# A two-layer decoder trunk on one core: two gate products of the second layer move into the gap between two attentions

## The chip, the cores and the metric

The kernel runs on one core of one Trainium2 chip. The time is device microseconds from start to end of one launch. Three runs of the kernel before took 914.35, 915.20 and 915.77 us; the median is 915.2 us. One further execution was recorded by the hardware profiler; all rows below come from it.

## The reference

Two layers run over 256 tokens of width 1024, in f32. Each layer has a mixer with three branches that are gated and summed, and a feed-forward part:

```
h = modulate(rms_norm(x, mix_norm_g), sh1, sc1)
z = h @ w_in      # MLA latents | MoBA q, k, v | conv input | 3 gates of 1024
o_a = causal_attention(q_full, k_full, v_a) @ w_mla_o          # 8 heads
o_b = moba_attention(q_b, k_b, v_b) @ w_moba_o                 # 8 heads of 64, rope
o_c = silu(layer_norm(causal_dwconv31(u))) @ w_conv_pw2 + b
g = sigmoid(gates)
x = x + g1 * ((g[0]*o_a + g[1]*o_b + g[2]*o_c) @ w_out)
h = modulate(rms_norm(x, ffn_norm_g), sh2, sc2)
x = x + g2 * channel_mixer(h, w_up, w_dw, w_down)
```

With 256 tokens and blocks of 256, MoBA has one block, so its attention is causal attention over 256 keys. The gates depend on `h` alone, so their products can run at any time after `h` is there. The convolution over 31 tokens also depends on `h` alone.

## The kernel before

Weights arrive as 128x1024 f32 tiles of 512 KB (a *unit*). SP issues the load; ACT copies the tile into `whi` in a shorter format (line 219) and DVE subtracts that from the original to get `wlo` (line 221). A product of two f32 matrices is then three products: `whi` with the high part of `h` (`hh`, line 297), `whi` with its low part (`hl`, line 298), and `wlo` with `hh` (line 300). One unit gives 8 + 8 + 8 = 24 matrix products of 128x256 on PE, accumulated in a PSUM bank. `raw`, `whi` and `wlo` have 4 buffers each; up to three units are split ahead of the one in use. PSUM banks: five of tag `psa`, three of `psb`.

The order of the mixer's work is written out by hand in the table `STEPS` (one string for each layer, line 77 on), as a list of short names. The instructions of a name are issued when it is reached, and the ones of neighbouring names are then interleaved on each engine when the program is built; the result is one fixed list for each engine, and each engine works through its list in order. The names that matter here:

- `C20`, `C21`: the two halves (units) of pair 2 of the third gate, 24 products each (`gate_c`); after the second half ACT takes the tanh (line 788). `C10`, `C11`, `C30`, `C31` are the pairs beside it.
- `G00`, `G01`, `G10`, ...: the same for the first two gates (`gate_ab`).
- `MA13`, `MA14`, ...: steps of the MLA attention of the second half of the heads; `BA00`..`BA03` and `BA10`..`BA13`: steps of the MoBA attention of the two halves of its heads. Both go through `attn4`: scores and mask on PE (lines 605, 607, 610, 613), maxima on DVE (619, 622, 628), exponentials on ACT (641), reciprocal on DVE (646), scaling on ACT (653), transposes on PE (662) with copies on ACT (665), products with the values on PE (674), and the output's high and low parts on ACT (677) and DVE (678).
- `BP0`, `BP1`: rope of the MoBA queries and keys of the two blocks of 128 tokens (`moba_prep`): DVE lines 965, 588, 589 and 972, then eight transposes on PE (line 976) into two banks and two copies on ACT (line 977) into `qkTb`. No MoBA score can be computed before both blocks are there.
- `O0`, `O1`, ...: output products of MLA and MoBA (`out_ab`), with `obl`, the low part of the MoBA output (line 678), in their last products; DVE lines 1126 and 1129 follow.
- `LN`: the mean of the convolution's output (`conv_mean`): three DVE sums (lines 1076 to 1078), one PE product (line 1079).
- `RW0`: the first rows of modulation weights for the feed-forward part: `crow` and the 512 KB tiles of `wmr`, each multiplied on DVE with `crow` (line 378) and reduced. These tiles use buffers that the attention has given up; the second one goes into `vb`, the buffer of the MoBA values, which is free once the last value product (line 674) has read it.

Beside these, the 31 taps of the convolution (DVE lines 1063 and 1066, four taps to a step, 32 steps) are not written in the table: the function `_spread` puts them between the marks `v0` and `v1`, evenly by the weights of `UNITS`, so they move when other names move. The step `m0`..`m1` is spread in the same way and lies ahead of the change.

Of the kernel before, what the change touches and what calls it, by code (L numbers as in the profile page):

```python
# [78 lines left out]
), (  # L79
    "GLU0 GLU1 GLU2 GLU3 KL0 KL1 KL2 KL3 KL4 KL5 KL6 KL7 LE0 LE1 LR0 QKV00 LR1 LT QKV01 UQ QKV02 UK QKV03 MS0 "  # L80
    "QKV10 QKV11 v0 QKV12 MS1 QKV13 QKV20 MP0 QKV21 QKV22 MP1 QKV23 BS0 m0 MA00 MA10 C00 MA01 BS1 MA02 C01 MA11 "
    "MA03 C10 MA04 MA12 m1 C11 MA13 BP0 BP1 MA14 BA00 C20 BA01 BA02 G00 BA10 BA03 G01 BA11 C21 G10 v1 "
    "BA12 C30 G11 C31 BA13 O0 O1 G20 RW0 LN G21 G30 RW1 RW2 RW3 G31 O2 G40 r0 G41 G50 O3 LS G51 LB G60 O4 O5 G61 "
    "OC0 G70 OC1 PR0 OC2 OC3 PR1 OC4 OC5 G71 O6 O7 PR2 OC6 PR3 OC7 PR4 r1 PR5 PR6 PR7 "
)]
# [1302 lines left out]
```

## Time and profile before

| | |
|---|---|
| median of three runs | 915.2 us |
| profiled execution | 912.66 us |
| its span, first to last instruction | 910.5 us |
| granted PE clock, mean | 0.988 |
| PE busy | 889.1 us (98%) |
| DVE busy | 797.0 us (88%) |
| ACT busy | 554.9 us (61%) |
| HBM read | 199.33 MB |

The span is the stretch that the trace covers; the launch takes 2.16 us more. A busy share of 98% says that PE hardly idles over the whole, and not that it runs at its full clock all the time: the granted clock is a column of its own. Times in the rows are us from the span's start; the second layer's attentions lie between 550 and 640 us.

### The profile page before, as it was taken

How to read it: one execution, taken by the hardware profiler on the slowest of the kernel's cores; microseconds unless marked ns; L12 is line 12 of the kernel's file. 1: busy time of each engine (PE TensorE's matmuls, PEld its weight loads, DVE VectorE, ACT ScalarE, POOL GpSimd, SP SyncE). 2: the span in 40 equal slices, each digit the busy share in tenths (PEclk: the TensorE clock that was granted, in tenths of full speed). 3: DMA queues.
4: the chain of work that ended last, by engine and by line, in shares of the span. 5: the costliest groups of instructions: out<-in, count | busy, mean ns of one | idle time of the engine just before them, and what ended most of it. 6: DMA issues, size and time to landing. Idle time of an engine off the chain costs nothing.

```text
span 910.5 us, 18569 instructions
## 1 busy us (share of the span) xinstructions
PE 889.1 (98%) x7261; PEld 840.1 (92%) x7261; DVE 797.0 (88%) x1553; ACT 554.9 (61%) x979; POOL 46.2 (5%) x36
## 2 busy tenths in 40 slices
PE   6999999999999999999999999899999999999998
PEld 5988888999997999999989989799999799999998
DVE  6989999999987999999775999898987798777774
ACT  4677598645756655556543776885575565565561
POOL 0010700000000000000000043000000000000000
PEclk9999999999999999999999999899999999999999
DMA  8965535699988889997634564156867677666631
GB/s 312 377 201 200 189 117 186 210 330 337 294 292 285 307 278 326 307 308 233 198 101 129 185 231 139 47 183 209 271 220 258 227 233 227 187 192 199 191 94 47
DMA packets 57976, 201.59 MB, mean 221 GB/s; under 512 B 6944, under 2 KB 8480, under 8 KB 57888
## 3 DMA queue, kind: packets, MB, share of 16 engines
q1 hardware_dynamic: 57888, 200.41, 65.5%
q8 instruction: 57, 0.93, 0.4%
q14 instruction: 31, 0.25, 0.1%
HBM read 199.33 MB, written 1.05 MB: 220 GB/s over the span
## 4 chain that ended last, share of the span: by engine, by line
PE 86%; DVE 6%; ACT 5%; issue 1%; DMA 1%; POOL 0%; SPq 0%; POOLq 0%; DVEq 0%; ACTq 0%
PE psb L297 18%; PE psb L298 17%; PE psb L300 17%; PE psa L297 7%; PE psa L298 7%; PE psa L300 7%; PE psa L395 2%; DVE wlo L221 2%; DVE raw L742 2%; ACT whi L219 1%; PE psa L674 1%; ACT p L641 1%; PE psa L607 1%; PE psa L662 1%; PE psa L291 1%
## 5 line engine op out<-in xcount | busy, mean ns | idle before, releaser
L219 ACT ACTIVATE whi<-raw 128x1024 fp32r<-128x1024 f32 (+2 forms) x286 | 296.3, 1042 | 201.8 <-PE psb L298 108.2
L221 DVE TENSOR_TENSOR wlo<-raw,whi 128x1024 fp32r<-128x1024 f32 (+2 forms) x286 | 339.5, 1192 | 59.7 <-ACT whi L219 52.0
L297 PE MATMUL psb<-hh,whi 128*128 128x256 f32 x1088 | 262.0, 282 | 0.1
L298 PE MATMUL psb<-hl,whi 128*128 128x256 f32 x1088 | 259.4, 280 | 0.0
L297 PEld LDWEIGHTS psb<-hh,whi 128*128 128x128 f32 x1088 | 204.5, 188 | 5.7 <-issue 4.6
L298 PEld LDWEIGHTS psb<-hl,whi 128*128 128x128 f32 x1088 | 204.6, 188 | 0.9 <-DVE e L569 0.8
L300 PE MATMUL psb<-hh,wlo 128*128 128x256 f32 x1088 | 148.5, 278 | 0.0
L300 PEld LDWEIGHTS psb<-hh,wlo 128*128 128x128 f32 x1088 | 135.1, 188 | 1.0 <-issue 1.0
L1066 DVE SCALAR_TENSOR_TENSOR cacc<-upad,cw,cacc 128x256 f32<-128x256 f32 x240 | 105.3, 474 | 0.5
L297 PE MATMUL psa<-mhl,whi 128*128 128x256 f32 x400 | 93.2, 276 | 0.0
L298 PE MATMUL psa<-mhl,whi 128*128 128x256 f32 x400 | 93.0, 277 | 0.0
L1263 DVE SCALAR_TENSOR_TENSOR e<-psb,fw,e 128x255 f32<-128x255 f32 (+1 forms) x176 | 83.4, 475 | 8.1 <-ACT e L1261 7.2
L504 POOL TENSOR_TENSOR rs<-rs,mhalf 128x8 f32<-128x8 f32 (+3 forms) x26 | 44.6, 1729 | 672.8 <-DVE rs L503 672.7
L297 PEld LDWEIGHTS psa<-mhl,whi 128*128 128x128 f32 x400 | 74.9, 188 | 0.1
L298 PEld LDWEIGHTS psa<-mhl,whi 128*128 128x128 f32 x400 | 74.9, 188 | 0.0
L1261 ACT ACTIVATE e<-psb,fb,fw 128x256 f32<-128x256 f32 x88 | 48.6, 552 | 29.4 <-DVE e L1263 25.8
L378 DVE SCALAR_TENSOR_TENSOR raw<-raw,crow 128x1024 f32<-128x1024 f32 x48 | 58.1, 1212 | 2.2 <-DMA raw<-in_wmr 2.2
L300 PE MATMUL psa<-mhl,wlo 128*128 128x256 f32 x400 | 53.5, 276 | 0.0
L300 PEld LDWEIGHTS psa<-mhl,wlo 128*128 128x128 f32 x400 | 49.1, 188 | 0.0
L297 PE MATMUL psb<-whi,hh 128*128 128x416 f32 (+1 forms) x96 | 31.9, 357 | 4.5 <-ACT hh L818 4.4
L1271 ACT ACTIVATE mhl<-e 128x256 fp32r<-128x256 f32 x44 | 18.3, 417 | 29.1 <-DVE e L1269 26.7
L298 PE MATMUL psb<-whi,hl 128*128 128x416 f32 (+1 forms) x96 | 30.7, 351 | 0.2 <-DVE hl L819 0.2
(271 smaller groups left out, 1472.5 us busy)
## 6 DMA issues: line engine op xcount, KB each, us to landing
raw<-in_wup SPq DMA_DIRECT2D x88, 512.0 KB, 4.8
raw<-in_wmr SPq DMA_DIRECT2D x60, 512.0 KB, 5.5
raw<-in_wdn SPq DMA_DIRECT2D x44, 512.0 KB, 4.5
raw<-in_wm SPq DMA_DIRECT2D x32, 512.0 KB, 4.4
raw<-in_wgab SPq DMA_DIRECT2D x32, 512.0 KB, 5.0
raw<-in_wqkv SPq DMA_DIRECT2D x24, 512.0 KB, 4.8
raw<-in_win SPq DMA_DIRECT2D x16, 512.0 KB, 4.6
raw<-in_wgc SPq DMA_DIRECT2D x16, 512.0 KB, 4.2
```

What stands on the lines that cost most here:

```text
L219: ac.activation(hi, raw, AF.Copy)
L221: ve.tensor_tensor(lo, raw, hi.bitcast(F32), op=ALU.subtract)
L297: te.matmul(o, p1[0], p1[1], start=start, stop=False)
L298: te.matmul(o, p2[0], p2[1], start=False, stop=False)
L300: te.matmul(o, p3[0], p3[1], start=False, stop=stop)
L378: ve.scalar_tensor_tensor(raw, raw, scale, row, op0=ALU.mult, op1=ALU.mult, accum_out=acc)
L395: te.matmul(acc[32 * c:32 * c + 32, 0:S], cact[:, k:k + 1].to_broadcast([P, 32]), raw[:, c * S:(c + 1) * S], start=(k == 0), stop=(k == KD ...
L504: gp.tensor_tensor(r, r, mhalf[:, :n], op=ALU.pow)
L1066: ve.scalar_tensor_tensor(aj, upad[:, j, t:t + S], cw[:, j * 31 + t:j * 31 + t + 1], aj, op0=ALU.mult, op1=ALU.add)
L1261: ac.activation(t, src, AF.Identity, scale=fw[:, 2, c:c + 1], bias=fb[:, c:c + 1])
L1263: ve.scalar_tensor_tensor(t[:, d:S], src[:, 0:S - d], fw[:, 2 - d, c:c + 1], t[:, d:S], op0=ALU.mult, op1=ALU.add)
L1271: ac.activation(mh, th, AF.Copy)
```

## The change

One line of the second layer's table is written anew. `C20` and `C21` were in the middle and at the end of the MoBA attention's steps; they are now between the last MLA steps and the first MoBA step, `C20` ahead of `BP1` and `C21` ahead of `BA00`. `BP1` is one step later, and `G00`, `G01`, `BA02`, `BA03` and `BA10` change places among themselves.

```diff
-    "MA03 C10 MA04 MA12 m1 C11 MA13 BP0 BP1 MA14 BA00 C20 BA01 BA02 G00 BA10 BA03 G01 BA11 C21 G10 v1 "
+    "MA03 C10 MA04 MA12 m1 C11 MA13 BP0 C20 BP1 MA14 C21 BA00 BA01 G00 BA02 BA10 G01 BA03 BA11 G10 v1 "
     "BA12 C30 G11 C31 BA13 O0 O1 G20 RW0 LN G21 G30 RW1 RW2 RW3 G31 O2 G40 r0 G41 G50 O3 LS G51 LB G60 O4 O5 G61 "
```

In PE's list, this is where the first MoBA block's transposes end (`mq_6883` and `mq_6885` are the two blocks, `psb_7547` is the bank of `C20` and `C21`, `whi_7300` and `whi_7386` are their units):

```order
 L976 MATMUL psa_7541<-ident,mq_6883 128x128 x4
-L976 MATMUL psa_7555<-ident,mq_6885 128x128 x4
-L605 MATMUL psb_7583<-qkTb_7526 128x128 x2
+L298 MATMUL psb_7547<-hl_6070,whi_7300 128x256
...
+L300 MATMUL psb_7547<-hh_6069,wlo_7301 128x256 x8
+L297 MATMUL psb_7547<-hh_6069,whi_7386 128x256
...
+L976 MATMUL psa_7590<-ident,mq_6885 128x128 x4
+L300 MATMUL psb_7547<-hh_6069,wlo_7387 128x256 x5
+L976 MATMUL psa_7596<-ident,mq_6885 128x128 x4
```

The second block's transposes and the first scores stood directly behind the first block's; now the products of `C20` and two thirds of those of `C21` stand between the two blocks.

Also in PE's list, further on, where the convolution's mean product stands (`psb_8150` is its bank, `psb_8117` that of `G20` and `G21`, `psb_8193` that of `G30`):

```order
 L300 MATMUL psb_8117<-hh_6069,wlo_8007 128x256 x8
-L1079 MATMUL psb_8150<-e_1396_8151,mean_w 128x256
 L297 MATMUL psb_8117<-hh_6069,whi_8052 128x256
...
 L300 MATMUL psb_8117<-hh_6069,wlo_8053 128x256 x8
+L1079 MATMUL psb_8150<-e_1396_8151,mean_w 128x256
 L297 MATMUL psb_8193<-hh_6069,whi_8086 128x256
```

The mean product stood between `G20` and `G21`; it now stands between `G21` and `G30`.

In DVE's list at the same place (`raw_8388` is the `wmr` tile in the buffer of the MoBA values, `e_1396_8151` the sum that the mean product reads, `cacc_6959` the convolution's output):

```order
-L1077 TENSOR_TENSOR e_1397_8152<-cacc_6959 128x256
-L1078 TENSOR_TENSOR e_1396_8151<-e_1396_8151,e_1397_8152 128x256
+L1066 SCALAR_TENSOR_TENSOR cacc_6959<-upad_6482,cw_4288,cacc_6959 128x256
 L678 TENSOR_TENSOR obl_6488<-psa_8035,obh_6487 128x512
...
+L378 SCALAR_TENSOR_TENSOR raw_8388,m_1446_8479<-raw_8388,crow_8148 128x1024
...
 L221 TENSOR_TENSOR wlo_8121<-raw_8118,whi_8120 128x1024
 L1129 TENSOR_TENSOR mq_8082<-b_1376_8002 128x256
+L1077 TENSOR_TENSOR e_1397_8152<-cacc_6959 128x256
+L221 TENSOR_TENSOR wlo_8164<-raw_8161,whi_8163 128x1024
+L1078 TENSOR_TENSOR e_1396_8151<-e_1396_8151,e_1397_8152 128x256
```

The sum was finished ahead of the MoBA output's low part and of the `wmr` tile's multiplication; it now comes behind both, with the tile's multiplication, which waits for a transfer, in front of it.

## Rows read from the trace of the kernel before

**Rows 1.** The page: shares of the chain that ended last, by engine.

```profile
PE 86%; DVE 6%; ACT 5%; issue 1%; DMA 1%; POOL 0%; SPq 0%; POOLq 0%; DVEq 0%; ACTq 0%
```

**Rows 2.** Busy time in stretches; columns as in its head.

```profile
core 0: us, PE busy (x) PEld busy (x) DVE busy (x) ACT busy (x) POOL busy (x), PEclk, DMA share, GB/s
579.00:585.45 6.45, 3.24 (x21) 2.23 (x21) 6.45 (x13) 6.45 (x16) 0.00 (x0) 1.00 0.02 4
585.45:593.65 8.20, 8.20 (x52) 6.57 (x53) 5.42 (x12) 2.62 (x4) 0.00 (x0) 0.58 0.33 108
593.65:614.27 20.62, 20.62 (x180) 18.88 (x177) 20.40 (x48) 18.76 (x54) 0.00 (x0) 1.00 0.55 177
614.27:627.50 13.23, 13.03 (x123) 12.33 (x122) 12.86 (x21) 9.88 (x17) 0.00 (x0) 1.00 0.64 208
627.50:637.50 10.00, 10.00 (x86) 9.95 (x86) 6.19 (x10) 3.19 (x3) 0.00 (x0) 1.00 0.65 215
```

**Rows 3.** Timeline of PE: start, us, engine, line, operation, [idle before <-releaser].

```profile
577.93 1.07 PE L300 MATMUL psb<-hh,wlo 128*128 128x256 f32 x8
579.07 2.20 PE L662 MATMUL psa<-ident,p 128*128 128x128 f32 x9
...
581.79 0.71 PE L976 MATMUL psa<-ident,mq 128*128 128x128 f32 x5
585.45 0.93 PE L976 MATMUL psa<-ident,mq 128*128 128x128 f32 x4 [2.94 <-ACT qkTb L977]
...
588.64 2.83 PE L674 MATMUL psa<-pT,kv 128*64 128x128 f32 x24
...
600.34 0.71 PE L605 MATMUL psb<-qkTb 64*128 64x128 f32 x4
...
603.50 0.37 PE L605 MATMUL psa<-qkTb 64*128 64x128 f32 x1
...
606.22 1.53 PE L674 MATMUL psa<-pT,vb 128*64 128x128 f32 x24
...
614.27 1.38 PE L662 MATMUL psa<-ident,p 128*128 128x128 f32 x10
...
634.32 0.60 PE L1079 MATMUL psb<-e,mean_w 128*128 128x256 f32 x2
636.59 1.07 PE L300 MATMUL psb<-hh,wlo 128*128 128x256 f32 x8
```

**Rows 4.** Timeline of ACT.

```profile
584.20 1.14 ACT L977 ACTIVATE qkTb<-psa 128x512 f32<-128x512 f32 x2
...
596.79 0.44 ACT L641 ACTIVATE p<-psa,nb,rs 128x128 f32<-128x128 f32 x1
...
600.70 2.89 ACT L653 ACTIVATE p<-p,ri 128x128 f32<-128x128 f32 x8
```

**Rows 5.** The chain of waits in order of time, two of its steps.

```profile
595.79 0.94 PE psb L300 x8
...
630.85 0.91 PE psb L300 x8
```

**Rows 6.** Timeline of DVE.

```profile
571.97 2.06 DVE L1066 SCALAR_TENSOR_TENSOR cacc<-upad,cw,cacc 128x256 f32<-128x256 f32 x5
...
580.08 2.49 DVE L965 TENSOR_TENSOR mq<-mq,tb 128x512 f32<-128x512 f32 x4
...
582.88 1.21 DVE L221 TENSOR_TENSOR wlo<-raw,whi 128x1024 fp32r<-128x1024 f32 x1
...
633.47 1.23 DVE L378 SCALAR_TENSOR_TENSOR raw<-raw,crow 128x1024 f32<-128x1024 f32 x1 [2.24 <-DMA raw<-in_wmr]
```

**Rows 7.** `wmr` transfers issued at 634.7, in 600 to 660, and at 626.4: us to landing.

```profile
raw<-in_wmr SPq DMA_DIRECT2D x1, 512.0 KB, 3.4
...
raw<-in_wmr SPq DMA_DIRECT2D x7, 512.0 KB, 4.9
...
raw<-in_wmr SPq DMA_DIRECT2D x1, 512.0 KB, 7.0
```

## The prediction

> **What bounds the kernel now.** First the page's chain of waits: 86% of it runs over PE, 6% over DVE, 5% over ACT [rows 1]. So a change counts by what it does to PE's line of work. Then the busy table by stretches, for the second layer around the change [rows 2]. Two stretches stand out. From 579.00 to 585.45 PE is busy for 3.24 of 6.45 us, at full clock, while DVE and ACT are busy all the time: PE waits for them. From 585.45 to 593.65 it is busy all the time but at 0.58 of its clock, that is, mostly at the lower of its two levels. From 593.65 on it is full at 1.00, with 0.20 us lost before 627.50. Last the timeline of PE, which says what that hole is [rows 3]: after `C11`'s last products (577.93) come only the transposes of one MLA step (L662) and of the first MoBA block (L976), and then nothing for 2.94 us, until ACT has copied a bank (L977) for the next transposes. ACT does that copy at 584.20 [rows 4]. The clock falls right after this idle time.
>
> The stretch from the end of `C11`, 578.84, to 593.65 is 14.81 us. At full clock its work is 12 L662 at 0.115 (the ten at 614.27 begin 0.12 apart), 16 L976 at 0.115 (five of them take 0.71), 24 value products in 1.50 (1.53 at 606.22, with 2.83 at the lower clock) and one set of scores in 3.25 (four score products and a mask some 0.78 from 600.34; the rest 603.50 to 606.22, less two transposes) [rows 3]: 1.38 + 1.84 + 1.50 + 3.25 = 7.97. So 6.84 us are lost there: 2.94 of idleness, 0.42 x 8.20 = 3.44 of clock, and 0.46 in transposes that wait for ACT's softmax.
>
> **What the change moves.** It adds and removes no arithmetic. `C20` and `C21` are 48 products of 128x256; eight such take 0.91 at full pace (0.1135 each) and 0.94 in the stretch after 593.65 (0.1175) [rows 5]. 48 x 0.1135 = 5.45 us of work that waits for nothing but weights already split goes into a stretch with 6.84 us to fill. I walk PE's new list with these durations.
>
> 1. From 578.84: `C20`'s 24 products, `C21`'s first 16, the 12 L662 and the first 8 L976: 2.72 + 1.82 + 1.38 + 0.92 = 6.84, to 585.7. The L662 and the copies that they wait for now have products in front of them. ACT's list is unchanged up to the copies of the first block at 584.20 [rows 4].
> 2. The second block's L976 wait for DVE, whose rope comes later: between the four L965 (580.08, 0.60 each) now stand convolution taps (0.40 each, from the five at 571.97) and a split (1.14 to the next) [rows 6]. Counting DVE's new list, the query half of the block is ready at 586.1. PE waits about 0.45; behind it stand `C21`'s last 8 products, so they wait too.
> 3. 8 L976, 8 products, L674: 586.1 + 0.92 + 0.91 + 1.50 = 589.5; the scores to 592.8. Before, the scores ended at 593.65, with 48 products fewer done: PE is now 0.85 + 5.45 = 6.3 us ahead.
> 4. `G00` and `G01` follow (599.05). The softmax of the first MoBA half stands on ACT behind a split that reads after `G00`: exponentials take 3.9 and scaling 2.8 us (596.79 to 600.70, and 2.89) [rows 4], so it ends at 602.5. `G10`'s first products cover part of that; value products end at 606.6, `G10` at 607.5. The same point of work was at 614.27 in before: 6.7 ahead, the rest being the 0.004 a product that the slower pace cost.
> 5. The second softmax starts at 607.9, where before it was 608.3, so it gains little itself; it ends at 615.5. `C30`, `G11`, `C31` with 72 products are there to cover it, as `C21` and others were. Last value products 619.2, `O0`, `O1` and the beginning of `G20` to 622.3, `obl` at 622.5. The remaining 68 products of 0.1135 end at 630.3.
> 6. There stands the convolution's mean product, moved behind `G21`. With 0.45 for itself the piece would end at 630.75; before it ended at 637.50, after the products at 636.59 [rows 3]. Gain without a wait: 6.75.
>
> **The new wait.** In before the mean product had its operand long ago (634.32 without a wait in front). Now its sum on DVE comes behind the multiplication of `raw_8388` (L378), and that waits for a transfer into the buffer of the MoBA values. The buffer is free when the last value products have read it, 619.2 by the walk, so SP issues it at 619.35. In before DVE waited 2.24 us for this same transfer [rows 6], but nothing on PE stood behind that. From L378's start to the end of the sum DVE has L378, taps, two L1126, two L1129 and three splits: 8.14 us by the durations of their rows. The landing is the unknown: `wmr` tiles took 3.4 at the shortest, 4.9 in the median of seven, and 7.0 for this very tile in before [rows 7]. I take the median, since the tile is issued at another place among other loads. Then DVE starts L378 at 624.25 and ends the sum at 632.4, and PE, there at 630.3, waits 2.1 us. Bounds: without any wait for the transfer DVE would start at 622.9, and PE wait 0.75; at 7.0 us it waits 4.2. All that stands behind the mean product on PE (`G30` and on) is late by it, and PE is full from there to the end, so nothing wins it back.
>
> What costs nothing: the loads of `C21`'s unit and of `G00`'s change places, all issued over 10 us before use while the DMA share is 0.02 in the hole [rows 2]; the tanh of the third gate (0.6 us on ACT) is wanted only by the outputs later on. If ACT's extra splits in 585 to 590 held up its copies, PE would lose at most the 1.1 us of a split (L219 and L221 alike, 1.21 at 582.88) [rows 6].
>
> Sum: 6.75 - 2.15 = 4.6 us. The profiled execution took 912.66 us, so 908.06 by its own measure; it is 2.5 us under the median of the runs, and I put the difference on the median: 915.2 - 4.6 = **910.6 us**.
>
> **A rule that speaks against it.** The granted clock is 1.00 while PE is only half busy, and falls behind the 2.94 us without any work [rows 2, 3]. So by the row short waits cost only their length. The Trainium skill, "TensorE: Matmul & The Clock Gate", section "A second HAM failure mode: psum-queue depth-cycling", says that frequent small idle times between groups of products are enough to make the clock swing between its two levels, and that the swings cost throughput. The half-busy stretch at 1.00 speaks against that here; by the rule the sum would be the one of the second rival below.
>
> **Rivals.**
> - *The wait at the mean product is hidden.* If the landing is short and DVE is ahead of my count by a microsecond (its list up to `obl` is 40 us of work with 1.7 us of waits that I added), the whole 6.75 stays: 908.45. For it: the shortest landing of 3.4. Against it: 8.14 us of DVE work stand behind the landing whatever it is.
> - *The clock falls all the same.* The waits of step 2 and the ACT waits of step 4 remain. If the clock falls once for as long as in before, 3.44 us are lost again: 4.6 - 3.44 = 1.2, 914.0. For it: PE still stops at the places where ACT holds it. Against it: each stop is a sixth of the 2.94 us.
> - *The mean product's wait takes the clock down: slower than before.* `raw_8388` lands as late as in before or later, 7.0 us: PE waits 4.2 us, longer than the 2.94 that went ahead of the fall at 585.45, and runs at the lower level behind it for 6.9 us, losing 3.44. 6.75 - 4.2 - 3.44 = -0.9: 916.1, and a landing at 8 us gives 917.1. It decides from a wait of 2.94 on, that is, a landing of 5.7. For it: the 7.0 of the same tile. Against: six of seven landings may be shorter, and the tile is no longer issued together with another load.
> - *The change doesn't fill the hole:* ACT's softmax, not missing work, sets the end of both attentions, as in step 5, where the second one begins only 0.4 us earlier. Then the products come out of the places where they covered softmax, and the hole opens there. With the 0.4 alone gained and 2.1 lost: 916.9. Against it: `C30`, `G11` and `C31` stand there, 72 x 0.1135 = 8.2 us against a softmax of 7.6.
>
> **Chances and range.** Forecast, a wait at the mean product between 0.75 and 2.9 (gain 3.8 to 6.0): 0.53. No wait (6 to 7): 0.11. A longer wait without a fall of the clock, or other small waits (gain 1.8 to 3.8): 0.15. The clock falls all the same: 0.09, most of it within 1.8 us of before. The mean product's wait with the clock: 0.07, half of it slower. The hole reopened: 0.05, nearly all slower. A difference under 0.2% (1.8 us) can't be told from none. Faster: 0.53 + 0.11 + 0.15 + 0.01 = 0.80; within: 0.12; slower: 0.08. The range leaves out no more than two in ten: from 908.4, the sum without a wait, to 913.4, a gain of 1.8.
>
> **What would show it.** Right: no idle time near 2.9 us and a granted clock of 1.00 between 579 and 593, with L297 and L298 of `C20` and `C21` there; the scores' masks end near 592.8; `G10` ends near 607.5; the mean product (L1079) with an idle time of 1 to 3 us in front of it, released by DVE's sum (L1078), around 630 to 633; L378 behind a DMA wait at 624. Wrong: an idle time over 1 us in front of L976 or L605; a clock under 1.00 in that stretch; value products (L674) that end after 608; or no idle time in front of L1079.

## The result and the profile after

The changed kernel took 911.34 us in the median of 18 runs (906.29 to 914.94), the kernel before 915.78 us in as many (911.92 to 919.36). The medians lie 4.4 us apart. The ratio is 0.9946, with a 95% interval from 0.9930 to 0.9962: 4.9 us faster, 3.5 to 6.4 by the interval. Run again beside other kernels it came to 0.9935 (0.9908 to 0.9961). The forecast was a gain of 4.6 us, to 910.6 us.

The profiled execution of after has a span of 910.1 us and took 912.17 us, just 0.5 us under that of before. A comparison of whole spans would hide the change, so the traces are compared here from a common point to a common point: from the end of `C11`, the last product ahead of the change, to the first product of `O2`, behind the mean product and `G31`. In before that is 578.84 to 642.94, 64.10 us; in after 580.59 to 639.10, 58.51 us: 5.6 us less. The other 5 us stand outside this stretch. Ahead of it, after reaches `C11`'s end 1.75 us later, with the same instructions up to there; it had a granted clock of 0.72 from 16 to 28 us, where before had 0.86, which is 1.7 us. Behind `O2` after takes 271.0 us and before 267.56: from 710 to 726 us the granted clock was 0.79 against 0.89, 1.6 us, and the rest is a slower pace that the last section shows.

The stretches of after that answer to [rows 2]: us, busy us of PE, PEld, DVE, ACT and POOL (instructions), granted clock, DMA share, GB/s.

```profile
580.63:593.42 12.79, 12.44 (x123) 11.60 (x121) 12.79 (x24) 11.41 (x22) 0.00 (x0) 1.00 0.29 93
593.42:608.75 15.33, 15.00 (x132) 13.15 (x129) 15.12 (x38) 12.91 (x33) 0.00 (x0) 1.00 0.61 197
608.75:622.00 13.25, 13.25 (x123) 12.64 (x122) 13.11 (x24) 12.78 (x34) 0.00 (x0) 1.00 0.62 207
622.00:636.00 14.00, 12.83 (x110) 12.56 (x109) 13.29 (x25) 6.25 (x9) 0.00 (x0) 1.00 0.78 248
```

From the end of `C11` to the end of the first scores, where before was half idle for 6.45 us and then spent 8.20 us at 0.58 of the clock, PE is now busy for 12.44 of 12.79 us at 1.00. What it still waits for in the whole stretch are three short waits (engine, bank, line, releaser: us in all, times, longest):

```profile
PE psb L1079 <- DVE mod L379: 1.2, 1, 1.2
PE psa L976 <- DVE mq L589: 0.4, 1, 0.4
PE psb L297 <- ACT p L641: 0.3, 1, 0.3
```

In PE's timeline, beside [rows 3]:

```profile
579.68 1.11 PE L300 MATMUL psb<-hh,wlo 128*128 128x256 f32 x8
...
587.95 0.63 PE L976 MATMUL psa<-ident,mq 128*128 128x128 f32 x4 [0.35 <-DVE mq L589]
...
589.53 1.53 PE L674 MATMUL psa<-pT,kv 128*64 128x128 f32 x24
...
593.28 0.38 PE L613 MATMUL psa<-maskb,identb 128*128 128x256 bf16 x2
...
607.70 1.21 PE L300 MATMUL psb<-hh,wlo 128*128 128x256 f32 x8
...
619.00 1.53 PE L674 MATMUL psa<-pT,vb 128*64 128x128 f32 x24
...
630.70 1.07 PE L300 MATMUL psb<-hh,wlo 128*128 128x256 f32 x8
632.94 0.67 PE L1079 MATMUL psb<-e,mean_w 128*128 128x256 f32 x2 [1.17 <-DVE mod L379]
```

The 2.94 us in front of L976 have become 0.35, the value products of the MLA step take 1.53 us and not 2.83, and there is a new idle time of 1.17 us in front of the mean product. What it waits for stands in DVE's timeline: the tile's multiplication behind its transfer, then 7.9 us from its start to the end of the sum, with other work in between.

```profile
624.82 1.23 DVE L378 SCALAR_TENSOR_TENSOR raw<-raw,crow 128x1024 f32<-128x1024 f32 x1 [0.71 <-DMA raw<-in_wmr]
...
632.38 0.42 DVE L1078 TENSOR_TENSOR e<-e,e 128x256 f32<-128x256 f32 x1
632.71 0.15 DVE L379 TENSOR_TENSOR mod<-m,modb 128x1 f32<-128x1 f32 x1
```

The waits name L379, which ended last, as releaser; the sum (L1078) that L1079 reads ended at 632.80, 0.06 us earlier. In the page's chain of waits the share of PE is smaller and that of DVE larger than in [rows 1]:

```profile
PE 81%; DVE 11%; ACT 3%; DMA 2%; issue 2%; POOL 0%; SPq 0%; POOLq 0%; DVEq 0%; ACTq 0%
```

### The profile page after: what moved, and what is told of

Same layout as the page of the kernel before. It is cut to its first block, busy times and chain, and to the rows that moved or that the text cites. A ratio compares the mean times of both kernels' runs of the same rounds, so it can differ in the third digit from the quotient of the medians.

```text
span 910.1 us, 18566 instructions
## 1 busy us (share of the span) xinstructions
PE 888.7 (98%) x7261; PEld 840.6 (92%) x7261; DVE 797.2 (88%) x1553; ACT 553.2 (61%) x979; POOL 46.2 (5%) x36
## 4 chain that ended last, share of the span: by engine, by line
PE 81%; DVE 11%; ACT 3%; DMA 2%; issue 2%; POOL 0%; SPq 0%; POOLq 0%; DVEq 0%; ACTq 0%
PE psb L297 16%; PE psb L298 16%; PE psb L300 16%; PE psa L297 8%; PE psa L298 8%; PE psa L300 7%; DVE wlo L221 3%; DVE cacc L1066 2%; PE psa L395 2%; PE psa L662 1%; ACT whi L219 1%; PE psa L674 1%; DVE raw L742 1%; PE psa L291 1%; PE psa L293 1%
```

## The experiments

"The stretch" is always that from `C11`'s end to `O2` in the profiled execution, and ratios are to the kernel before, with their 95% intervals. All edits are in the second layer's order, unless a diff shows more, and a diff shows only the part of a line that changes. The name of a run stands in brackets. c20_only and spare24 are edits of the kernel before; the others start from the changed kernel.

**The changed kernel again, and before again.** Each gave a second trace.

> The changed kernel once more, as the yardstick of this group. Both theories: about 4.9 us under before (ratio 0.9946). In its profile the clock is 1.00 from C11's end to the first scores, and the mean product (L1079) waits about 1.2 us. If the profile again shows a longer stretch at a lower clock around 715 to 735 than before did, that stretch belongs to this kernel; if not, it is chance.

Measured: 0.9935 (0.9908 to 0.9961), stretch 58.92 us, and a wait of 1.78 us in front of L1079, at a clock of 1.00 throughout. Behind `O2` it takes 270.59 us: long again. The clock from 710 to 726 us was 0.79 again, against 0.89 in the first trace of before and 1.00 in the second (next run). By the test set here that belongs to this kernel, but two traces don't settle it: the kernel of g_fill below, with the same steps behind `O2`, had 1.00 there.

> The kernel before once more, for a second trace. If the 1.4 to 3.4 us by which all traces since were longer behind O2 belong to the change, this trace is as short there as the first one (267.6 us); if they are chance, it can be as long as the others (269 to 271). In the gap it shows again an idle time of about 2.9 us and the clock's fall.

Measured: stretch 62.90 us, behind `O2` 268.16 us. The idle time is back at 2.88 us, and the clock falls behind it, but for a shorter time than in [rows 2]:

```profile
580.84:587.40 6.56, 3.40 (x23) 2.23 (x21) 6.56 (x13) 6.56 (x16) 0.00 (x0) 1.00 0.03 9
587.40:588.00 0.60, 0.60 (x5) 0.43 (x5) 0.60 (x2) 0.60 (x1) 0.00 (x0) 1.00 1.09 369
588.00:592.00 4.00, 4.00 (x32) 3.49 (x33) 3.31 (x7) 1.37 (x3) 0.00 (x0) 0.57 0.16 61
592.00:594.00 2.00, 2.00 (x22) 1.43 (x17) 0.98 (x2) 0.60 (x1) 0.00 (x0) 1.00 0.29 74
```

0.43 of 4.00 us is 1.7 us, and not the 3.44 us of the first trace. So the fall in the gap was there in both executions, but its length differed, and with it a quarter (1.7 of 6.84 us) of the loss that the forecast counted on. The two traces of each kernel put the gain in the stretch at 4.0 to 5.6 us.

**Only `C20` moves (c20_only).**

```diff
-BP0 BP1 MA14 BA00 C20 BA01 BA02 G00 BA10 BA03 G01 BA11 C21 G10
+BP0 C20 BP1 MA14 BA00 BA01 BA02 G00 BA10 BA03 G01 BA11 C21 G10
```

> Only C20 (24 products, 2.7 us) moves between BP0 and BP1; C21 and the rest of the order stay as before. Theory of the idle time: the 2.94 us of idleness go, and with them the fall of the clock (3.4 us), so the gain is 5 to 6 us and the clock stays at 1.00. Rival, that only the amount of work moved into the hole counts: 2.7 us, half of what both halves can give, and some clock loss stays.

Measured: 0.9974 (0.9956 to 0.9992), 2.4 us; stretch 61.84 us. The number is the rival's, though not for its reason. The clock does hold in the gap, but two waits are new:

```profile
PE psb L605 <- ACT p L641: 2.1, 1, 2.1
PE psb L605 <- ACT qkTb L977: 1.3, 1, 1.3
```

The first of these is the scores of the second MoBA half, which wait for a PSUM bank that the first half's exponentials still read. `C20` no longer stands in front of them. But DVE's and ACT's timelines show that the exponentials are late themselves:

```profile
594.50 0.20 DVE L628 SCALAR_TENSOR_TENSOR nb<-mx,rs 128x4 f32<-128x4 f32 x1
...
596.04 1.06 ACT L1186 ACTIVATE th<-crow 128x1024 f32<-128x1024 f32 x1 [4.77 <-DMA crow<-in_crow]
597.01 0.44 ACT L641 ACTIVATE p<-psa,nb,rs 128x128 f32<-128x128 f32 x1
```

The maxima that the first of them needs (L628) are there at 594.70. ACT's list has the tanh of `crow` (L1186) in front, and that waits 4.77 us for its transfer, so they begin 2.3 us later, which is more than PE's whole wait. By this count the hole is the tanh's work at least as much as the missing cover's; no run takes the two apart for this kernel. And here, behind 2.10 us of idleness, the clock falls:

```profile
598.00:601.00 3.00, 0.90 (x8) 0.70 (x7) 1.90 (x6) 3.00 (x14) 0.00 (x0) 1.00 0.01 4
601.00:604.00 3.00, 3.00 (x19) 2.88 (x18) 2.81 (x7) 3.00 (x10) 0.00 (x0) 0.62 0.00 0
604.00:608.00 4.00, 4.00 (x26) 2.66 (x25) 2.65 (x7) 2.49 (x5) 0.00 (x0) 0.86 0.42 131
```

0.38 x 3.00 + 0.14 x 4.00 = 1.7 us are lost. A hole has opened at the MoBA softmax, where the prediction's last rival put it. In the changed kernel the waits in the two places are 0.35 and 0.33 us: there `C21` is moved too, `G00` and `G01` are rearranged, and the tanh of `crow` stands behind the softmax. The runs with `BP1` below show what the tanh does.

> A second trace of c20_only. Its first one had an idle time of 2.10 us at 600.55 and the clock fell behind it for some 3.5 us. If the work in this place decides, it falls again; if it is chance, it may hold, and the stretch is about 1.7 us shorter than 61.8.

Measured: a wait of 1.85 us in the same place, with ACT's tanh waiting 4.52 us ahead of the exponentials, and the clock falls again (0.50 from 604 to 606); stretch 61.41 us.

**The gap filled with products that are of no use (spare24).** Nothing of before moves; 24 products are added whose result isn't read. ACT's and DVE's lists are the same as in before.

```diff
+        def spare_products(n):
+            pp = psb()
+            for i in range(8 * n):
+                te.matmul(pp[:, 0:S], hh[:, i % KD, 0:P], hh[:, i % KD, :], start=(i == 0), stop=(i == 8 * n - 1))
...
-BP0 BP1 MA14
+BP0 X3 BP1 MA14
```

> Before, with 24 extra products of 128x256 whose result nobody reads, put between BP0 and BP1; no other work moves. Theory of the idle time: the extra 2.7 us lie in the 2.94 us of idleness and cost nothing, the clock stays at 1.00 and the kernel is about 3 us faster than before though it does more work. Rival, that the gain of the change is only the work that was moved early: no gain, 0 to 2.7 us slower.

Measured: 0.9978 (0.9960 to 0.9997), 2.0 us faster with 2.7 us more work on PE; stretch 61.66 us. The clock holds in the gap, though PE is still idle for 1.29 us there:

```profile
579.00:584.00 5.00, 5.00 (x46) 4.92 (x45) 5.00 (x10) 5.00 (x13) 0.00 (x0) 1.00 0.00 0
584.00:586.00 2.00, 0.71 (x7) 0.53 (x6) 2.00 (x5) 2.00 (x5) 0.00 (x0) 1.00 0.27 96
586.00:590.00 4.00, 4.00 (x47) 3.31 (x46) 3.73 (x8) 2.20 (x4) 0.00 (x0) 1.00 0.28 99
```

PE's two waits that count here are these:

```profile
585.62 0.63 PE L976 MATMUL psa<-ident,mq 128*128 128x128 f32 x4 [1.29 <-ACT qkTb L977]
...
598.13 0.71 PE L605 MATMUL psb<-qkTb 64*128 64x128 f32 x4 [0.95 <-ACT p L641]
```

The second block's transposes start 6.55 us after `C11`'s end (585.62 in this trace), and 6.61 in before: as the theory had it, the products cost nothing, for ACT sets the end of the gap. From there to `O2` PE takes 55.11 us, and 57.49 and 56.34 in the two traces of before. The clock lost 3.4 and 1.7 us there, and a wait of 0.95 us in front of L605 is new. So the 2.0 us by which this kernel is faster (0.3 to 3.7, where the theory had 3) are the clock's, and the gain of the change isn't the moved work alone. The run doesn't split the change's 4.9 us, because it has half as many products in the gap and takes none away elsewhere.

**Other products in the gap (g_fill).** `G00` and `G01` change places with `C20` and `C21`.

```diff
-BP0 C20 BP1 MA14 C21 BA00 BA01 G00 BA02 BA10 G01 BA03
+BP0 G00 BP1 MA14 G01 BA00 BA01 C20 BA02 BA10 C21 BA03
```

> The changed order with G00 and G01 in the gap instead of C20 and C21, and these at the places of G00 and G01. Theory, that any 48 ready products do it: the same as the changed kernel, ratio to before 0.994, no fall of the clock in the gap. Rival, that it matters that the third gate's products leave the MoBA steps (their bank, their tanh on ACT): at least 2 us slower than the changed kernel.

Measured: 0.9934 (0.9908 to 0.9959), stretch 58.39 us, waits of 0.31, 0.35 and 1.08 us in the three places of after. 48 ready products of another gate do it as well; that it is the third gate plays no part.

**The mean product later (ln_later).**

```diff
-G20 RW0 LN G21 G30 RW1
+G20 RW0 G21 G30 LN RW1
```

> The changed kernel with LN traced behind G30 instead of ahead of G21, so that the mean product stands later in PE's list. Theory of the new wait: the idle time in front of L1079 goes (1.2 us), and the time is about 1 us under the changed kernel, ratio to before 0.9935. Rival, that this wait is hidden by later waits (the layer norm ends later): the same time as the changed kernel, and an idle time of about 1 us later on.

Measured: 0.9930 (0.9906 to 0.9954); stretch 57.98 us against 58.51 and 58.92, and 0.46 us of wait in front of L1079 against 1.17 and 1.78. In the traces a wait that is shorter by 0.71 and 1.32 us shortens the stretch by 0.5 and 0.9 us, so most of it is paid for. The times of the two kernels can't be told apart, so they don't decide against the rival.

**The mean product's wait made longer (sum_slow).** The sum passes through DVE twice more, in the changed kernel.

```diff
                 ve.tensor_tensor(s[0], s[0], s[1], op=ALU.add)
+                for _ in range(2 * l):
+                    ve.tensor_scalar(s[0], s[0], 1.0, None, op0=ALU.mult)
```

> The changed kernel with the sum for the second layer's mean product passed twice more through DVE (multiplied by 1), which with the two instructions that come between makes it some 3.0 us later. The idle time in front of L1079 grows to 4.2 to 4.8 us. If a wait costs only its length: the stretch from C11's end to O2 grows by 3.0 us, ratio 0.998. If a wait longer than about 2 us also brings the clock down, as the third rival of the prediction had it: a stretch at the lower clock behind it and another 2 to 3.4 us, ratio 1.000 to 1.0015.

Measured: 1.0006 (0.9988 to 1.0024), so the whole gain is gone; stretch 62.57 us. PE waits 3.77 us (L1081 is the mean product here), and then the clock falls:

```profile
633.80:637.55 3.75, 0.00 (x0) 0.03 (x1) 3.75 (x10) 0.66 (x2) 0.00 (x0) 1.00 0.73 261
637.55:638.50 0.95, 0.94 (x6) 0.90 (x7) 0.95 (x1) 0.00 (x0) 0.00 (x0) 1.00 0.80 285
638.50:640.50 2.00, 2.00 (x12) 2.00 (x11) 2.00 (x9) 1.08 (x3) 0.00 (x0) 0.55 0.69 250
640.50:642.50 2.00, 2.00 (x12) 2.00 (x12) 0.99 (x2) 1.27 (x2) 0.00 (x0) 0.60 0.84 285
```

0.45 x 2.00 + 0.40 x 2.00 = 1.7 us are lost by the clock, and 2.0 to 2.6 us by the longer wait; the stretch is 3.65 to 4.1 us longer than in the two traces of after. The prediction's slower rival is a real mechanism: the wait cost its length, and the clock half of the 3.44 us that the rival put on it. In the two traces of the changed kernel, with waits of 1.17 and 1.78 us, the clock held.

**`BP1` back directly behind `BP0` (bp_early).**

```diff
-BP0 C20 BP1 MA14 C21 BA00
+BP0 BP1 C20 MA14 C21 BA00
```

> The changed kernel with BP1 back directly behind BP0. Theory, that BP1's delay serves nothing and only makes its transposes wait for DVE: the 0.35 us in front of L976 go; and since DVE's list then has the sum for the mean product ahead of raw_8388's multiplication, the 1.2 to 1.8 us in front of L1079 go too; 1.5 to 2 us under the changed kernel, ratio 0.9925. Rival, that BP1's delay is needed (the rope would hold up DVE's splits): slower than the changed kernel by 0.5 us or more.

Measured: 0.9971 (0.9945 to 0.9996), stretch 59.77 us: the theory's two waits do shrink (L976 0.19 us, L1079 none), but 3.30 us are new, in front of the first product of `G10`, whose bank the first MoBA half's exponentials hold:

```profile
PE psb L297 <- ACT p L641: 3.3, 1, 3.3
PE psa L976 <- ACT qkTb L977: 0.2, 1, 0.2
```

So the theory's gain did not come, and the time is nearer to the rival's. But the rope isn't the cause either. ACT's timeline shows what held the exponentials up: the tanh of `crow` (L1186), which in this order stands ahead of them, as it does in c20_only and in before (a wait of 2.55 us there), and waits 5.52 us for its transfer. In after, the second block of lines, it stands behind them and waits for nothing.

```profile
598.32 1.07 ACT L1186 ACTIVATE th<-crow 128x1024 f32<-128x1024 f32 x1 [5.52 <-DMA crow<-in_crow]
599.29 1.05 ACT L219 ACTIVATE whi<-raw 128x1024 fp32r<-128x1024 f32 x1
600.24 0.44 ACT L641 ACTIVATE p<-psa,nb,rs 128x128 f32<-128x128 f32 x1
```

```profile
596.79 0.46 ACT L641 ACTIVATE p<-psa,nb,rs 128x128 f32<-128x128 f32 x1 [0.17 <-DVE nb L628]
...
607.53 1.06 ACT L1186 ACTIVATE th<-crow 128x1024 f32<-128x1024 f32 x1
```

**That tanh behind the softmax (bpe_crow).** bp_early, with the tanh queued behind the first gate's. `gate_i` holds that gate's tanh; the line that keeps it there is left out.

```diff
...
-                ac.activation(th, crow1[0], AF.Tanh, scale=0.5)
+                with tc.issue_after(gate_i[0].ins) if l else ExitStack():
+                    ac.activation(th, crow1[0], AF.Tanh, scale=0.5)
```

> bp_early (BP1 directly behind BP0) with one thing more: ACT's tanh of crow, which waits for a transfer, is queued behind the tanh of the first gate, and so behind the first MoBA softmax. Theory, that in bp_early the 3.30 us in front of L297 came from this tanh, which stood ahead of the softmax in ACT's list and waited 5.52 us for crow: the 3.30 us go, and the stretch from C11's end to O2 is 58 to 59 us, like the changed kernel's. Rival, that BP1's early place itself costs it (the rope takes DVE's time): a wait of 2 us or more stays in front of L297.

Measured: 0.9964 (0.9943 to 0.9985), stretch 58.44 us. The 3.30 us are 0.76:

```profile
PE psb L1079 <- DVE mod L379: 1.1, 1, 1.1
PE psb L297 <- ACT p L641: 0.8, 1, 0.8
PE psa L976 <- ACT qkTb L977: 0.2, 1, 0.2
```

In the traces the theory holds: the tanh that waits for its transfer was the cause of the 3.30 us. The times don't show it, 0.9964 against 0.9971; a wait of 1.1 us in front of L1079 has come back. The stretch is as long as in after, so by the traces `BP1`'s delay costs and gives next to nothing by itself; what it did for the change was to come out with ACT's tanh in a harmless place.

> bpe_crow with LN traced behind G30. If the short waits (L976, L1079) are all that is left, the stretch from C11's end to O2 is 57.5 us and the ratio to before 0.992 to 0.993, the fastest of all; if something else takes their place, as fast as the changed kernel.

Measured: 0.9959 (0.9943 to 0.9976), stretch 58.91 us, and not 57.5: a wait of 1.12 us in front of L1079 stays, since DVE's sum moved with it. None of the versions is measurably faster than the changed kernel.

> A second trace of bp_early. Its first one had an idle time of 3.30 us on PE without a fall of the clock. If the length of the wait decides, the clock holds again; if it is chance when it falls, it may fall this time, and the stretch is 1.5 to 3.4 us longer than 59.8.

Measured: a wait of 3.67 us in the same place, and this time the clock falls (0.50 from 602 to 604, 0.65 to 606), where the first trace showed 1.00 behind 3.30 us; stretch 61.59 us, 1.8 us longer. The two waits aren't equally long, so this pair alone doesn't rule out that the length decides; the falls behind 1.85 and 2.10 us in c20_only do.

```profile
602.00:604.00 2.00, 2.00 (x12) 2.00 (x11) 2.00 (x4) 2.00 (x7) 0.00 (x0) 0.50 0.47 147
604.00:606.00 2.00, 2.00 (x13) 1.83 (x11) 1.89 (x5) 1.08 (x4) 0.00 (x0) 0.65 0.72 197
```

## Why the prediction was right, step by step

- **The bound and the mechanism** held: an idle PE in the gap and a lower clock behind it. The experiment with useless products shows that the clock is a term of its own, and the one with `G00` and `G01` that the products needn't be the third gate's. Of the prediction's signs of being wrong none showed: the wait in front of L976 was 0.35 us, there was none in front of L605, and the clock was 1.00.
- **Steps 1 and 2** held closely. From `C11`'s end, the second block's transposes were to start after 7.3 us behind a wait of 0.45; they started after 7.36 us (587.95 - 580.59) behind 0.35.
- **Step 3** was too slow by 1.1 us: the scores were to end at 592.8, and ended at 593.42 - 1.75 = 591.7 on before's scale. The mis-sized term is the set of scores: I took 3.25 us from a set that was interleaved with waiting transposes, and it took 1.9 us (591.54 to 593.42 in after) where nothing interrupts it. So the loss in before was larger than 6.84 us by 1.35. Most of that lay in the 20 transposes ahead of the idle time, which took 3.67 us for 2.30 at full pace (578.84 to 585.45, less 2.94): 1.37 us of waiting for ACT, where the prediction had 0.46.
- **Steps 4 and 5** came out 0.4 to 0.5 us early: on before's scale, 1.75 us less than in the rows of after, `G10` ended at 607.0 (forecast 607.5), the last value products at 618.7 (619.2), `G21` at 629.9 (630.3). Some 0.6 of the 1.1 us of step 3 were lost again up to `G10`'s end, 0.33 of them as the wait for the exponentials in front of `G10`. The walk doesn't name the tanh of `crow`, on whose place in ACT's list this rests, as bp_early shows.
- **The new wait** is there, with the sum and the transfer as its cause, and smaller: 1.17 and 1.78 us for a forecast of 2.1. `raw_8388` landed in 4.2 us in the first trace of after and in 4.9, the forecast's value, in the second; the chain on DVE behind it took 7.9 us (624.82 to 632.71) for 8.14. That nothing behind it wins much of the time back fits the stretches of ln_later and sum_slow.
- **The clock's 3.44 us** was one execution's value; the second trace of before gives 1.7. This error makes the forecast gain too large; the ones in the scores and in the new wait make it too small. That they nearly cancel, so that the sum of 4.6 lies so close to 4.9, is luck. The forecast was right in its mechanism, and closer in its number than its terms were.
- **The rivals.** The clock did not fall all the same: 1.00 in both traces of after. The slower rival was made to happen with a wait of 3.77 us. Its point of decision, a wait of 2.94 us, did not hold: the clock fell behind 1.85 and 2.10 us in c20_only, and held behind 3.30 us in bp_early. The rival that the hole reopens in the other attention is what c20_only and bp_early show, though with a cause that it didn't name: the exponentials stood behind the tanh of `crow`. The change escaped it by the place that this tanh came to; what the rearranged `G00` and `G01` add isn't shown by itself.

## What to carry to other kernels

Look for the stretch in which the bounding engine idles while its clock is granted in full, and see whether the clock falls right behind it: work that is ready can be moved in there, and it pays twice. Before moving it, ask which wait it had been hiding where it was, and read the new lists of the other engines for an instruction that waits for a transfer ahead of something urgent. When the gain is half a percent, compare traces from one common instruction to another, and take the clock's part from more than one execution.

## What the runs showed of the hardware

- **The length of a wait doesn't tell whether the clock falls.** It fell behind idle times of 2.94 and 2.88 us (before), 2.10 and 1.85 (c20_only), 3.77 (sum_slow) and 3.67 (bp_early, second trace). It held behind 3.30 (bp_early, first trace), 1.78 and 1.17 (after) and 1.29 (spare24). What decides between 1.8 and 3.7 us is not settled by these runs.
- **PE has a slightly slower pace at a granted clock of 1.00.** Eight products take 1.07 us in some stretches and 1.10 in others, and 24 products take 2.72 or 2.82 us. From about 738 to 788 us twelve of fourteen traces, of all the kernels, have the slower pace; the first trace of before and the second of bp_early have the faster one. In before's first trace, and then in its second:

```profile
747.04 1.07 PE L300 MATMUL psb<-hh,wlo 128*128 128x256 f32 x8
749.76 1.07 PE L300 MATMUL psb<-hh,wlo 128*128 128x256 f32 x8
```

```profile
746.71 1.10 PE L300 MATMUL psb<-hh,wlo 128*128 128x256 f32 x8
749.53 1.10 PE L300 MATMUL psb<-hh,wlo 128*128 128x256 f32 x8
```

Over 50 us that is some 1.8 us, more than a third of what this change gains, and it belongs to no kernel: before and bp_early each have one trace of either kind. It is part of why the spans of single traces say so little here. Its cause is open.
